# Attention values as plain fp32 matmuls in two column halves of the array, instead of split fp32r pairs

## The chip, the core and the metric

The kernel runs on one core of a Trainium2 chip. The core has a matmul engine (TensorE: PE in the profile, PEld for its weight loads), a vector engine (VectorE, DVE), a scalar engine (ScalarE, ACT), GpSimd (POOL) and a queue engine that here only issues transfers (SyncE, SP). Matmuls read SBUF and accumulate in PSUM banks of 512 fp32 columns. The metric is device time of one execution in microseconds (us), the median of three runs. The profile comes from one more execution, whose own time is given beside it.

## The reference, cut to what matters

One decoder layer on 512 positions: an input projection, two token mixers, two branch projections merged by gates, an output projection and a layer norm. The part that is changed is in mixer A, an attention with 8 heads in two groups (a group shares keys and values, 64 wide). With 512 positions, 8 selected blocks of 64 and a window of 512, both the selected-block branch and the window branch are plain causal attention, each with its own keys, values and gate:

```python
ss = jnp.einsum('bghqd,bgqld->bghql', qr, ksel) * scale
ps = masked_softmax(ss, msel[:, :, None])
o_slc = jnp.einsum('bghql,bgqld->bghqd', ps.astype(vsel.dtype), vsel)
...
sw = jnp.einsum('bghqd,bgkd->bghqk', qr, kw) * scale
pw = masked_softmax(sw, mw)
o_win = jnp.einsum('bghqk,bgkd->bghqd', pw.astype(vw.dtype), vw)
return gt[..., 0:1] * o_cmp + gt[..., 1:2] * o_slc + gt[..., 2:3] * o_win
```

So for each query tile of 128 positions the result is a sum over both branches and over all key tiles up to its own, of probabilities times values, with the gate multiplied into the probabilities.

## The kernel before, in words

Almost all matmuls take operands in fp32r, a form that the array takes at the full rate. Accuracy is kept by splitting each operand into a high part (a cast to fp32r, on ScalarE) and a low part (the difference, on VectorE) and by running two or three matmuls per product. The weights are streamed: `load` (L256) brings a raw 128x1024 block by an SP transfer into a pool of two buffers `wraw`, `weights` (L272) makes `whi` on ScalarE and `wlo` on VectorE, and `proj` (L318) runs 24 matmuls of 512 columns into a bank `pa`.

What isn't projection is written as Python generators. `_Weave` (L98) advances all of them by a tick after every six projection matmuls, and each `yield n` is a wait of n ticks. The numbers are in the table `D`. A tick only fixes the order in which instructions are written; every engine then runs its own instructions in that order, as fast as its inputs come. SP also issues its transfers in the order written, and a transfer that waits holds back those behind it.

The attention is cut into six units (L694), written u0 to u5 below: query tile 3 with branch 0 and with branch 1 (u0, u1), query tile 2 likewise (u2, u3), query tile 1 with both (u4), query tile 0 with both (u5). For each unit:

- `attn_scores` (L698): matmuls of queries and keys into banks `pss` and `pst`, in two halves of two heads a group (the halves are called a and b below), then on VectorE the masked scores and their row extreme (L729).
- `soften` (L737): exponentials with row sums on ScalarE (L745), reciprocal and gate on VectorE (L750, L753), and the probabilities multiplied by gate over sum, half of them on VectorE (L763) and half on ScalarE (L761).
- VectorE transposes 32x32 blocks into the one buffer `big` (L773), and 16 SP transfers of 32 partitions each (L784) exchange the blocks into the buffer `turn`, after which the keys lie on the partitions.
- `values` (L791), once for each pair of branch and key tile, 20 times in all: the block of `turn` is split (cast on ScalarE L200, difference on VectorE L202), and four matmuls of 512 columns, high and low part for each of two column blocks `ab`, go into two banks `pso`. The values `vv` are a fp32r array in which the 64 high and the 64 low columns of a group lie side by side; a matmul multiplies these 128 columns by the high or the low probabilities of that group, so that a bank holds the two parts of one group's result in two halves of its partitions.
- after the last pair of a query tile the halves are added up by copies on ScalarE (L810) and additions on VectorE (L814 to L817) into `asum`.

`turn` has one buffer, so the transfers of a unit wait until the matmuls of the unit before have read it (L777). `weave.claim` keeps two generators from taking the matmul engine in adjacent ticks. The compressed branch (`cmp_hidden`, `cmp_kv`, `cmp_scores`) runs beside it; its hidden layer (L567) is 32 plain fp32 matmuls with 64 weight columns each, two at a time in the two column halves of the array (weight columns 0 to 63 and 64 to 127), in two visits of 16.

Of the kernel before, what the change touches and what calls it, by code (L numbers as in the profile page):

```python
# [9 lines left out]
F32 = mybir.dt.float32  # L10
# [8 lines left out]
P = 128  # L19
# [19 lines left out]
SEQ = "kcmp kslc v q0 q1 q2 q3 kwin vcmp zb0 zb1 zb2 zb3 za0 za1 za2 za3".split()  # L39
# [10 lines left out]
def _columns(name):  # L50

    c = np.arange(_COLS[name], _COLS[name] + 128)
    if name[0] == "q" and name[1] != "b" or name[:2] == "za":
# [16 lines left out]
D = dict(h0=6, h2=5, h3=14, h4=0, h5=7, h6=10, n0=5, n1=2, n2=7, c0=2, c1=0, c2=0, c3=4, r0=5, p0=1, p1=13, p2=0,  # L70
         s0=1, s2=11, s3=0, v0=1, v1=11, v2=5, v3=9, e0=4, e1=2, t0=5, t1=4, t2=5, t3=3, t4=0, a5=4, y=2, w0=3, w1=1,
         x0=0, x1=0, e2=0, e3=3, o0=0, o1=6, o2=0)
D.update({"x0.za0": 2, "o0.0": 1, "t2.5": 4, "w0.35": 0, "y.m.1": 0, "o0.7": 1, "e3.2.2": 2, "y.o.3": 6, "o1.1": 3,
# [57 lines left out]
def layer_kernel(ctx: ExitStack, tc: tile.TileContext, xT, xn, w0, wi, wf, wv, small, brow, consts,  # L131
# [20 lines left out]
    t4 = ctx.enter_context(tc.tile_pool(name="t4", bufs=3))  # L152
    big = ctx.enter_context(tc.tile_pool(name="big", bufs=1))
    turn = ctx.enter_context(tc.tile_pool(name="turn", bufs=1))
# [8 lines left out]

    def T4():
        return t4.tile([P, 1024], F32R, name="t4", tag="t4")
# [138 lines left out]
    vv = cst.tile([P, 4, 2, 256], F32R, name="vv")  # L304
# [77 lines left out]
    def values_of(tt, ps):  # L382
        v = T2(NV)
        V.tensor_tensor(v, ps[:, 0:NV], brv, ALU.add)
        yield D["y"]
        vd = vv[:, tt].rearrange("p b (g c) -> p b g c", c=64)
        v4 = v[:, 0:256].rearrange("p (b g c) -> p b g c", b=2, c=64)
        G.tensor_copy(gat[:, tt], v[:, 256:NV])
        vts.append(vv[:, tt])
        yield from split_steps(v4, vd[:, :, 0:4:3], vd[:, :, 1:3], "v", tt)  # L390
# [170 lines left out]
    def cmp_kv():  # L561
# [5 lines left out]
        for j in range(16):  # L567
# [3 lines left out]
            if j == 7:  # L571
                yield 1
# [122 lines left out]
    turned, spent, finished, accs = [0], [0], [0], {}  # L695
# [41 lines left out]
    def soften(u, ms, ts, mn, den):  # L737
# [16 lines left out]
        for odd in range(2):  # L754
            for ab in range(2):
                for z, m in enumerate(ms):
                    for x in range(nb):
                        c, h = slice(n * x, n * x + n), (ab * nm + z) * nb + x
                        if z % 2 == odd:
                            if odd:  # L760
                                A.mul(ts[m, ab][:, c], ts[m, ab][:, c], den[:, h:h + 1])  # L761
                            else:
                                V.tensor_scalar(ts[m, ab][:, c], ts[m, ab][:, c], den[:, h:h + 1], None, ALU.mult)  # L763
            if odd == 0:
                yield wait_of("e3", u, ms[0])
# [9 lines left out]
        if ms[-1] == 3:  # L775
            yield wait_of("t3", u)
            while spent[0] < u:  # L777
                yield 1
# [12 lines left out]
    def values(u, st, lo):  # L791
# [5 lines left out]
        if (br, j) == (0, 0):  # L797
            accs[i] = PO(), PO()
# [5 lines left out]
        if st == (i + 1) * len(brs) - 1:  # L804
            spent[0] += 1
# [386 lines left out]
```

## Time and profile before

| what | value |
|---|---|
| median of three runs | 415.39 us (414.49 to 415.79) |
| the profiled execution's own time | 415.07 us |
| its span in the profile | 413.3 us |
| TensorE | 405.7 us busy, 98% of the span |
| VectorE | 313.5 us busy, 76% |
| ScalarE | 238.6 us busy, 58% |
| granted TensorE clock | 0.998 |

The page lists busy time by engine, then the costliest groups of instructions by line. A group's line reads: line, engine, operation, out<-in, shapes, count, busy time, mean duration of one in ns, idle time before it and what ended that. Matmul durations overlap, since the next starts before the last has drained, so a matmul's price is read from the distance between starts. A plain fp32 matmul leaves two records in the trace, a fp32r matmul one.

### The profile page before, as it was taken

The page shows a single profiled execution, that of the slowest core. Times are in us where ns is not written, and L with a number is a line of the kernel's source. Part 1 is how long each engine was busy: PE and PEld are TensorE (multiplying, and loading weights), DVE is VectorE, ACT ScalarE, POOL GpSimd, SP SyncE. Part 2 cuts the span into 40 slices and gives each one's busy share as a digit, 9 for nine tenths or more (in the row PEclk, how much of TensorE's full clock was granted, in tenths as well). Part 3 has the DMA queues.
Part 4 walks back from the last instruction along what each step waited for, and adds up shares of the span by engine and source line. Part 5 has one row for each costly group of instructions (what it writes and reads, how often), then busy time and mean ns, then how long its engine had stood idle before and what let it go on. Part 6 is the DMA issues. An engine that isn't in the chain of part 4 may idle for free.

```text
span 413.3 us, 5929 instructions
## 1 busy us (share of the span) xinstructions
PE 405.7 (98%) x2047; PEld 332.5 (80%) x2047; DVE 313.5 (76%) x641; ACT 238.6 (58%) x466; POOL 5.0 (1%) x18
## 2 busy tenths in 40 slices
PE   8999999999999999999999999999999999999994
PEld 8888888899888877877877777778878888888884
DVE  5916499878477688989998987589783899882773
ACT  4445552624247576767678595577864777637211
POOL 2000000001000000000000000000000000000000
PEclk9999999999999999999999999999999999999999
DMA  8965800333223424861166370655865752045131
GB/s 263 375 232 204 295 21 14 119 100 104 74 80 105 127 76 126 214 198 51 52 164 193 99 208 0 173 184 138 221 194 165 263 196 101 0 118 188 39 114 52
DMA packets 26542, 58.26 MB, mean 141 GB/s; under 512 B 5264, under 2 KB 7184, under 8 KB 26512
## 3 DMA queue, kind: packets, MB, share of 16 engines
q1 hardware_dynamic: 26080, 57.49, 44.8%
q8 instruction: 16, 0.26, 0.3%
q10 hardware_dynamic: 432, 0.39, 0.3%
q14 instruction: 14, 0.11, 0.1%
HBM read 42.12 MB, written 2.10 MB: 107 GB/s over the span
## 4 chain that ended last, share of the span: by engine, by line
PE 89%; DVE 5%; SPq 3%; issue 1%; ACT 1%; DMA 1%; DVEq 0%; ACTq 0%
PE pa L139 58%; PE pss L139 15%; PE pso L139 11%; PE pst L139 5%; SPq L146 3%; DVE turn L202 2%; DVE big L773 2%; DMA turn<-big 1%; ACT t L200 1%; PE pst L143 0%; DVE big L1111 0%; DVE wlo L277 0%; DVE asum L833 0%; ACT t L1106 0%; DVE big L1108 0%
## 5 line engine op out<-in xcount | busy, mean ns | idle before, releaser
L139 PE MATMUL pa<-t,whi 128*128 128x512 f32 x640 | 199.4, 393 | 0.0
L139 PEld LDWEIGHTS pa<-t,whi 128*128 128x128 f32 x640 | 118.6, 188 | 29.5 <-issue 5.3
L139 PE MATMUL pa<-t,wlo 128*128 128x512 f32 x320 | 124.7, 390 | 0.0
L277 DVE TENSOR_TENSOR wlo<-wraw,whi 128x1024 fp32r<-128x1024 f32 x44 | 53.4, 1216 | 26.8 <-ACT whi L274 25.8
L139 PEld LDWEIGHTS pa<-t,wlo 128*128 128x128 f32 x320 | 60.1, 188 | 12.8
L274 ACT CAST whi<-wraw 128x1024 fp32r<-128x1024 f32 x44 | 45.9, 1047 | 34.6 <-PE pa L139 16.6
L745 ACT ACTIVATE t<-t,sm_mn 128x512 f32<-128x512 f32 (+3 forms) x64 | 35.2, 551 | 11.9 <-DVE sm_mn L729 11.9
L139 PE MATMUL pso<-t,t 128*128 128x512 f32 (+2 forms) x158 | 33.0, 346 | 0.0
L139 PE MATMUL pss<-t,t 128*128 128x512 f32 (+2 forms) x158 | 30.2, 324 | 0.0
L773 DVE STREAM_TRANSPOSE big<-t 128x512 f32<-128x512 f32 (+2 forms) x48 | 25.8, 590 | 5.3 <-DMA turn<-big 3.4
L139 PEld LDWEIGHTS pso<-t,t 128*128 128x128 f32 x158 | 25.5, 194 | 3.7
L202 DVE TENSOR_TENSOR turn<-turn,t 128x1024 fp32r<-128x1024 f32 x20 | 23.4, 1208 | 6.1 <-ACT t L200 6.1
L139 PE MATMUL pa<-t,t 128*128 128x512 f32 (+1 forms) x104 | 27.3, 368 | 0.0
L139 PEld LDWEIGHTS pss<-t,t 128*128 128x128 f32 x158 | 23.8, 190 | 2.8
L200 ACT CAST t<-turn 128x1024 fp32r<-128x1024 f32 x20 | 20.0, 1051 | 8.7 <-DMA turn<-big 4.5
L139 PEld LDWEIGHTS pa<-t,t 128*128 128x128 f32 x104 | 18.5, 189 | 3.1
L200 ACT CAST t<-t 128x512 fp32r<-128x512 f32 x16 | 9.9, 617 | 18.7 <-DVE t L1003 11.4
L139 PE MATMUL pa<-turn,t 128*128 128x512 f32 x64 | 19.9, 389 | 0.0
L139 PE MATMUL pss<-t,whi 128*128 128x512 f32 x64 | 19.7, 389 | 0.0
L761 ACT ACTIVATE t<-t,sm_dn 128x512 f32<-128x512 f32 (+3 forms) x32 | 15.7, 554 | 5.4 <-DVE sm_dn L753 5.3
L729 DVE CUSTOM_DVE_ANT_0 t<-pss,t 128x512 f32<-128x512 f32 (+3 forms) x32 | 14.1, 485 | 4.8 <-PE pss L139 4.6
L139 PE MATMUL pso<-turn,vv 128*128 128x512 f32 x40 | 16.5, 412 | 0.7 <-DVE turn L202 0.6
(198 smaller groups left out, 564.0 us busy)
## 6 DMA issues: line engine op xcount, KB each, us to landing
wraw<-in_wf_dram SPq DMA_DIRECT2D x38, 512.0 KB, 3.7
turn<-big SPq DMA_DIRECT2D x48, 128.0 KB, 2.4
wraw<-in_wbr_dram SPq DMA_DIRECT2D x8, 512.0 KB, 4.3
t<-in_wout_dram SPq DMA_DIRECT2D x16, 256.0 KB, 4.3
t<-t SPq DMA_DIRECT2D x48, 64.0 KB, 2.0
turn<-big SPq DMA_DIRECT2D x32, 96.0 KB, 2.2
t<-in_wi_dram SPq DMA_DIRECT2D x8, 256.0 KB, 5.0
big<-in_w_dram SPq DMA_DIRECT2D x8, 256.0 KB, 6.7
```

The lines of the kernel that those rows point to most:

```text
L139: return tc.keep_in_program_order(nc.tensor.matmul(*a, **k))
L146: tc.keep_in_program_order(nc.sync.dma_start(o, i))
L200: A.copy(dst_hi, src)
L202: V.tensor_tensor(dst_lo, src, dst_hi.bitcast(F32), ALU.subtract)
L274: A.copy(hi, raws[i])
L277: V.tensor_tensor(lo, raws[i], hi.bitcast(F32), ALU.subtract)
L729: V.tensor_tensor_reduce(out=p[:, c], in0=dsts[m, ab][:, c], in1=amask[:, 512 - n:512], op0=ALU.add, op1=ALU.min, scale=-0.125, scalar=3.0e38,
L745: A.activation(p[:, c], p[:, c], AF.Exp, bias=mn[:, h:h + 1], scale=-1.0, accum_out=den[:, h:h + 1])
L761: A.mul(ts[m, ab][:, c], ts[m, ab][:, c], den[:, h:h + 1])
L773: V.transpose(view[:, :, :, 4 * ab + m], ts[m, ab][:, 0:128 * nst].rearrange("p (c b s) -> p c b s", b=4, s=32))
```

## The change

The values are kept as they are in plain fp32, and so are the turned probabilities. Both splits, the arrays `vv` and `t4`, and the two-bank sums go. `values` runs once a query tile, four times in all, over all its pairs of branch and key tile: for each pair two plain fp32 matmuls with 64 weight columns, group 0 into partitions 0 to 63 and group 1 into partitions 64 to 127 of one bank. That bank is then added to `asum` by one VectorE instruction, or copied there by ScalarE for the first query tile. `turn` gets two buffers, and the transfers of a unit wait for the matmuls of the unit before the last.

Three other things change with it. The multiplication of the probabilities by gate over sum can be shared out by a number `g`, and as `g` is set all of it is on ScalarE. The hidden layer of the compressed branch runs in one visit. The projection of `vcmp` comes ahead of `kwin`, and the table `D` of waits has other numbers (two of its lines are shown).

```diff
-SEQ = "kcmp kslc v q0 q1 q2 q3 kwin vcmp zb0 zb1 zb2 zb3 za0 za1 za2 za3".split()
+SEQ = "kcmp kslc v q0 q1 q2 q3 vcmp kwin zb0 zb1 zb2 zb3 za0 za1 za2 za3".split()
...
-D = dict(h0=6, h2=5, h3=14, h4=0, h5=7, h6=10, n0=5, n1=2, n2=7, c0=2, c1=0, c2=0, c3=4, r0=5, p0=1, p1=13, p2=0,
+D = dict(h0=6, h2=5, h3=14, h4=1, h5=7, h6=10, n0=5, n1=1, n2=6, c0=2, c1=5, c2=0, c3=3, r0=5, p0=1, p1=17, p2=0,
...
-    t4 = ctx.enter_context(tc.tile_pool(name="t4", bufs=3))
-    turn = ctx.enter_context(tc.tile_pool(name="turn", bufs=1))
+    turn = ctx.enter_context(tc.tile_pool(name="turn", bufs=2))
...
-        vd = vv[:, tt].rearrange("p b (g c) -> p b g c", c=64)
-        v4 = v[:, 0:256].rearrange("p (b g c) -> p b g c", b=2, c=64)
         G.tensor_copy(gat[:, tt], v[:, 256:NV])
-        vts.append(vv[:, tt])
-        yield from split_steps(v4, vd[:, :, 0:4:3], vd[:, :, 1:3], "v", tt)
+        vts[tt] = v
...
-            if j == 7:
-                yield 1
...
-        for odd in range(2):
-            for ab in range(2):
-                for z, m in enumerate(ms):
-                    for x in range(nb):
-                        c, h = slice(n * x, n * x + n), (ab * nm + z) * nb + x
-                        if z % 2 == odd:
-                            if odd:
-                                A.mul(ts[m, ab][:, c], ts[m, ab][:, c], den[:, h:h + 1])
-                            else:
-                                V.tensor_scalar(ts[m, ab][:, c], ts[m, ab][:, c], den[:, h:h + 1], None, ALU.mult)
-            if odd == 0:
-                yield wait_of("e3", u, ms[0])
+        parts_ = [(m, ab, slice(n * x, n * x + n), (ab * nm + z) * nb + x)
+                  for ab in range(2) for z, m in enumerate(ms) for x in range(nb)]
+        share = len(parts_) * wait_of("g", u, ms[0]) // 8
+        for m, ab, c, h in parts_[:share]:
+            V.tensor_scalar(ts[m, ab][:, c], ts[m, ab][:, c], den[:, h:h + 1], None, ALU.mult)
+        yield wait_of("e3", u, ms[0])
+        for m, ab, c, h in parts_[share:]:
+            A.mul(ts[m, ab][:, c], ts[m, ab][:, c], den[:, h:h + 1])
...
-            while spent[0] < u:
+            while spent[0] < u - 1:
                 yield 1
...
-            for st in range(nst):
-                part = w[:, 0:1024 * nst].rearrange("p (a c x) -> p c a x", a=4, x=256)[:, st]
-                weave.start(values(u, st, part), wait_of("t4", u) * st)
-
-    def values(u, st, lo):
-        i, brs = units[u]
-        br, j = brs[st // (i + 1)], st % (i + 1)
-        hi = T4().rearrange("p (a x) -> p a x", a=4)
-        yield from split_steps(lo.bitcast(F32), hi, lo, "u", u)
-        yield wait_of("t2", u)
-        if (br, j) == (0, 0):
-            accs[i] = PO(), PO()
-        for ab in range(2):
-            for k, t in enumerate((hi, lo)):
-                T.matmul(accs[i][ab], vts[j][:, br, 128 * ab:128 * ab + 128],
-                         t[:, :, 128 * ab:128 * ab + 128],
-                         start=(br, j) == (0, 0) and k == 0, stop=(br, j) == (1, i) and k == 1)
...
+            probs[u] = w.bitcast(F32)[:, 0:1024 * nst].rearrange("p (a c x) -> p c a x", a=4, x=256)
+            if brs[-1] == 1:
+                yield from values(u)
+
+    def values(u):
+        i = units[u][0]
+        yield from weave.claim(D["t2"])
+        tiles = [(v, st) for v in (u - 1, u) if units[v][0] == i for st in range(len(units[v][1]) * (i + 1))]
+        acc = PO()
+        for n, (v, st) in enumerate(tiles):
+            br, j = units[v][1][st // (i + 1)], st % (i + 1)
             for ab in range(2):
-                own, other = slice(64 * ab, 64 * ab + 64), slice(64 - 64 * ab, 128 - 64 * ab)
-                A.copy(o[own], acc[ab][other])
...
+                r = slice(64 * ab, 64 * ab + 64)
+                T.matmul(acc[r], vts[j][:, 128 * br + 64 * ab:128 * br + 64 * ab + 64],
+                         probs[v][:, st, :, 128 * ab:128 * ab + 128], start=n == 0, stop=n == len(tiles) - 1)
+        spent[0] = u + 1
+        acc = acc.rearrange("p (a m s) -> p a m s", a=4, m=4)
+        dst = asum[:, :, 128 * i:128 * i + 128].rearrange("p m (a s) -> p a m s", a=4)
+        if "sum" in ready:
+            V.tensor_tensor(dst, dst, acc, ALU.add)
+        else:
+            A.copy(dst, acc)
+        finished[0] += 1
```

Where instructions go can be seen in each engine's written order, before and after. On TensorE, around the first visit of the values (the operand `turn` or, before, also `vv`; `t_952` to `t_1066` are the values of the four key tiles; `pa` rows are projection matmuls), before:

```order
L139 MATMUL pa<-t_300,whi 128x512
L139 MATMUL pa<-t_299,wlo 128x512
L139 MATMUL pso<-t_1984,vv 128x512
L139 MATMUL pso<-turn,vv 128x512
L139 MATMUL pso<-t_1984,vv 128x512
L139 MATMUL pso<-turn,vv 128x512
L139 MATMUL pa<-t_114,whi 128x512
```

and now:

```order
L142 MATMUL pa<-t_199,wlo 128x512
L142 MATMUL pso<-turn,t_952 64x512 x2
L142 MATMUL pso<-turn,t_982 64x512 x2
L142 MATMUL pso<-turn,t_1014 64x512 x2
L142 MATMUL pso<-turn,t_1066 64x512 x2
L142 MATMUL pso<-turn,t_952 64x512 x2
L142 MATMUL pso<-turn,t_982 64x512 x2
L142 MATMUL pso<-turn,t_1014 64x512 x2
L142 MATMUL pso<-turn,t_1066 64x512 x2
L142 MATMUL pa<-t_224,whi 128x512
```

Four matmuls for one pair of branch and key tile, with projections before and behind, have become two plain fp32 matmuls for each of eight pairs in one row, between the same projections.

On SP, around the transfers of u1 (`turn_2169` before, `turn_2090` now; x16 are the sixteen transfers of a unit, `wraw` rows are weight loads), before:

```order
L146 DMA turn_1787<-big_1239 32x1024 x16
L146 DMA wraw_1816<-in_wf_dram 128x1024
L146 DMA wraw_1896<-in_wf_dram 128x1024
L146 DMA t2_1968<-in_consts_dram 128x512
L146 DMA wraw_1979<-in_wf_dram 128x1024
L146 DMA wraw_2042<-in_wf_dram 128x1024
L146 DMA wraw_2132<-in_wf_dram 128x1024
L146 DMA turn_2169<-big_1239 32x1024 x16
L146 DMA wraw_2220<-in_wf_dram 128x1024
```

and now:

```order
L149 DMA turn_1779<-big_1305 32x1024 x16
L149 DMA wraw_1804<-in_wf_dram 128x1024
L149 DMA wraw_1887<-in_wf_dram 128x1024
L149 DMA t2_1935<-in_consts_dram 128x512
L149 DMA wraw_1957<-in_wf_dram 128x1024
L149 DMA wraw_2055<-in_wf_dram 128x1024
L149 DMA turn_2090<-big_1305 32x1024 x16
L149 DMA wraw_2143<-in_wf_dram 128x1024
```

The transfers of u1 stand one weight load earlier, right behind `wraw_2055`, which takes the buffer that `wraw_1887` had.

On VectorE that buffer is given free by the row that makes `wlo_2123` (`t2_1989` to `t2_1995` are the masked scores of u2's half a, `t2_1980` and `t2_2014` belong to the compressed branch). From the row that follows the masked scores:

```order
L201 TENSOR_TENSOR t2_1894<-t2_1443,t2_1893 128x512
L669 STREAM_TRANSPOSE t2_2014<-t2_1934 128x512
L885 SCALAR_TENSOR_TENSOR t2_1985<-t2_1986,t2_1985 128x512
L670 TENSOR_REDUCE sm_mx_2015<-t2_2014 128x16
L677 TENSOR_REDUCE sm_mx_1981<-t2_1980 128x16
L671 TENSOR_TENSOR t2_2014<-t2_2014,sm_mx_2015 128x512
L678 RECIPROCAL sm_mx_1981<-sm_mx_1981 128x16
L885 SCALAR_TENSOR_TENSOR t2_1937<-t2_1938,t2_1937 128x512
L680 TENSOR_TENSOR sm_mx_1981<-sm_mx_1981,gc_369 128x4x4
L743 RECIPROCAL sm_dn_1961<-sm_dn_1961 128x4
L276 TENSOR_TENSOR wlo_2123<-wraw_1887,whi_2035 128x1024
```

That row now stands behind the masked scores of u2's half a and behind both reductions of the compressed branch; before, it stood ahead of those masked scores.

More of the change, by code (lines that the diff above doesn't have):

```diff
@@ L67 @@
     0, 128, 256, 260, 772, 1284, 1796, 2308, 2820)
-D = dict(h0=6, h2=5, h3=14, h4=0, h5=7, h6=10, n0=5, n1=2, n2=7, c0=2, c1=0, c2=0, c3=4, r0=5, p0=1, p1=13, p2=0,
-         s0=1, s2=11, s3=0, v0=1, v1=11, v2=5, v3=9, e0=4, e1=2, t0=5, t1=4, t2=5, t3=3, t4=0, a5=4, y=2, w0=3, w1=1,
-         x0=0, x1=0, e2=0, e3=3, o0=0, o1=6, o2=0)
-D.update({"x0.za0": 2, "o0.0": 1, "t2.5": 4, "w0.35": 0, "y.m.1": 0, "o0.7": 1, "e3.2.2": 2, "y.o.3": 6, "o1.1": 3,
[18 rows of a table removed]
+D = dict(h0=6, h2=5, h3=14, h4=1, h5=7, h6=10, n0=5, n1=1, n2=6, c0=2, c1=5, c2=0, c3=3, r0=5, p0=1, p1=17, p2=0,
+         s0=6, s2=8, s3=0, v0=0, v1=11, v2=5, v3=7, e0=4, e1=2, t0=5, t1=9, t2=4, t3=4, a5=4, y=2, w0=3, w1=0, x0=0,
+         x1=0, e2=0, e3=1, g=0, o0=0, o1=4, o2=0)
+D.update({"x0.za0": 2, "o0.0": 1, "w0.35": 0, "y.m.1": 0, "o0.7": 2, "y.o.3": 5, "o1.1": 3, "h2.0": 4, "w0.11": 2,
[21 rows of a table added]
 def wait_of(step, *at):
@@ L162, in T2 @@
         return t2.tile([P, n], dt, name="t2", tag="t2")
-    def T4():
-        return t4.tile([P, 1024], F32R, name="t4", tag="t4")
     def BIG():
@@ L302, in layer_kernel @@
     kcB = cst.tile([P, 32], F32, name="kcB")
-    vv = cst.tile([P, 4, 2, 256], F32R, name="vv")
     asum = cst.tile([P, 4, 512], F32, name="asum")
@@ L694, in layer_kernel @@
     units = [(i, brs) for i in range(3, -1, -1) for brs in (((0,), (1,)) if i >= 2 else ((0, 1),))]
-    turned, spent, finished, accs = [0], [0], [0], {}
+    turned, spent, finished, probs = [0], [0], [0], {}
     blocks = []
@@ L786, in soften @@
             yield wait_of("t1", u)
-            for st in range(nst):
-                part = w[:, 0:1024 * nst].rearrange("p (a c x) -> p c a x", a=4, x=256)[:, st]
-                weave.start(values(u, st, part), wait_of("t4", u) * st)
-    def values(u, st, lo):
-        i, brs = units[u]
-        br, j = brs[st // (i + 1)], st % (i + 1)
-        hi = T4().rearrange("p (a x) -> p a x", a=4)
-        yield from split_steps(lo.bitcast(F32), hi, lo, "u", u)
-        yield wait_of("t2", u)
-        if (br, j) == (0, 0):
-            accs[i] = PO(), PO()
-        for ab in range(2):
-            for k, t in enumerate((hi, lo)):
-                T.matmul(accs[i][ab], vts[j][:, br, 128 * ab:128 * ab + 128],
-                         t[:, :, 128 * ab:128 * ab + 128],
-                         start=(br, j) == (0, 0) and k == 0, stop=(br, j) == (1, i) and k == 1)
-        if st == (i + 1) * len(brs) - 1:
-            spent[0] += 1
-        if (br, j) == (1, i):
-            acc, o = accs[i], T2()
-            for ab in range(2):
-                own, other = slice(64 * ab, 64 * ab + 64), slice(64 - 64 * ab, 128 - 64 * ab)
-                A.copy(o[own], acc[ab][other])
-                s, t = (x.rearrange("p (a m s) -> p a m s", a=4, m=4) for x in (o, acc[ab]))
-                dst = asum[own, :, 128 * i:128 * i + 128].rearrange("p m (a s) -> p a m s", a=4)
-                if "sum" in ready:
-                    V.tensor_tensor(o[own], o[own], acc[ab][own], ALU.add)
-                    V.tensor_tensor(dst, dst, s[own], ALU.add)
-                else:
-                    V.tensor_tensor(dst, s[own], t[own], ALU.add)
-            finished[0] += 1
@@ L851, in layer_kernel @@
     oa = [None] * 4
-    vi, vts, wis = [], [], []
+    vi, vts, wis = [], {}, []
     bri, brv = T2(), T2(NV)
@@ L891, in cmp_tile @@
         yield from cmp_hidden(a, de)
-    qraw = []
+    qraw = {}
     def q_tile(m, ps, b):
-        qraw.append(evac(ps, b))
+        qraw[m] = evac(ps, b)
         yield from queries(m, qraw[m])
@@ L936, in layer_kernel @@
             weave.start(z_tile(name, ps, m), wait_of("x0", name))
-    wo, woraw = [], {}
+    wo, woraw = {}, {}
     def load_out(kt):
@@ L970, in split_out @@
             V.scalar_tensor_tensor(lo, raw, nm, hi.bitcast(F32), ALU.add, ALU.subtract)
-        wo.append(hl)
+        wo[kt] = hl
     def out_ahead(n):
```

39 rows, old and new, of tables (x0, x1) are left out of this document.

## Prediction

> **What bounds the kernel now.** I read the busy times first, then what TensorE waits for, then one stretch of the middle.
>
> ```profile
> PE 405.7 (98%) x2047; PEld 332.5 (80%) x2047; DVE 313.5 (76%) x641; ACT 238.6 (58%) x466; POOL 5.0 (1%) x18
> ...
> PE pso L139 <- DVE t L212: 1.1, 1, 1.1
> PE pso L139 <- DVE turn L202: 0.6, 2, 0.4
> ...
> 186.00:235.00 49.00, 48.60 (x257) 37.05 (x242) 47.05 (x94) 35.02 (x62) 0.00 (x0) 1.00 0.37 104
> ```
>
> The second and third rows are all that TensorE waits for: 1.1 us at the start and 0.6 us for the low halves of turned blocks. The last gives busy time between 186 and 235 us: TensorE 48.60 of 49, VectorE 47.05, ScalarE 35.02. So the end is the sum of the matmuls' prices plus small waits, but from 186 to 235 VectorE has only 2 us to spare and can become the bound at any wait for its result. Time off VectorE or ScalarE counts only where it ends a TensorE wait; time off TensorE counts fully, unless a new wait takes it back. Prices come from distances of starts. In the chain of waits:
>
> ```profile
> 195.80 1.13 PE pso L139 x4
> ...
> 199.68 0.93 PE pso L139 x4
> ...
> 205.69 0.74 PE pss L139 x6
> 206.42 0.53 PE pst L139 x6
> ...
> 283.91 16.35 PE pa L139 x72
> ```
>
> A projection matmul costs 16.35/72 = 0.227 us, four values matmuls 0.93, twelve score matmuls 0.74 + 0.53 = 1.27.
>
> **Values before.** 20 times four matmuls at 0.93 is 18.6. Beside that come waits for the low half:
>
> ```profile
> 230.46 0.40 PE L139 MATMUL pso<-t,vv 128*128 128x512 f32 x1
> 231.26 0.50 PE L139 MATMUL pso<-turn,vv 128*128 128x512 f32 x1 [0.40 <-DVE turn L202]
> 231.59 0.39 PE L139 MATMUL pso<-t,vv 128*128 128x512 f32 x1
> ...
> 251.58 0.40 PE L139 MATMUL pso<-t,vv 128*128 128x512 f32 x1
> 252.00 0.50 PE L139 MATMUL pso<-turn,vv 128*128 128x512 f32 x1
> ...
> 274.58 0.40 PE L139 MATMUL pso<-t,vv 128*128 128x512 f32 x1
> 275.15 0.50 PE L139 MATMUL pso<-turn,vv 128*128 128x512 f32 x1 [0.17 <-DVE turn L202]
> ...
> 302.90 0.40 PE L139 MATMUL pso<-t,vv 128*128 128x512 f32 x1
> 303.37 0.50 PE L139 MATMUL pso<-turn,vv 128*128 128x512 f32 x1
> ```
>
> The four distances are 0.80, 0.42, 0.57 and 0.47 instead of 0.23, so 1.34 too long; the matmul after each restart starts 0.11 late (231.26 to 231.59), 0.44 in all; a visit right behind scores takes 1.13 (the row at 195.80), 0.2 more, and for this and the like I count 0.6. Sum: 18.6 + 1.3 + 0.4 + 0.6 = 20.9, say 21.
>
> **Values after.** There are 20 pairs of plain fp32 matmuls, one in each column half, of 512 columns. The trace has no such pair; the two nearest rows:
>
> ```profile
> 150.54 0.40 PE L139 MATMUL pa<-t,wlo 128*128 128x512 f32 x1
> 150.87 1.97 PE L139 MATMUL pss<-big,t 128*64 128x128 f32 x32
> 152.77 0.73 PE L139 MATMUL pa<-t,whi 128*128 128x512 f32 x2
> 153.34 0.39 PE L139 MATMUL pa<-t,wlo 128*128 128x512 f32 x1
> ...
> 185.44 1.09 PE L139 MATMUL pss<-t,kcB 64*32 64x512 f32 x16
> 186.46 0.72 PE L139 MATMUL pa<-t,whi 128*128 128x512 f32 x2
> ```
>
> The first visit is the hidden layer: 32 records are 16 matmuls, eight pairs in column halves with 128 columns each, from start to the next start 1.90. The second is eight fp32 matmuls of 512 columns, all beside each other in eight tiles, 1.02. I take a visit as a fixed part S plus c for each 128 columns of what runs after each other: 1.90 = S + 8c and 1.02 = S + 4c give c = 0.22 and S = 0.14. A pair of 512 columns is then 4c = 0.88. Each visit adds S, and what the rows show beside it: 0.10 at its entry (150.54 to 150.87 instead of 0.23) and 0.11 at its exit (152.77 to 153.34 instead of 0.46), 0.35 in all, four times: 1.4. So 20 × 0.88 + 1.4 = 19.0. Bounds for the pair: below, if entry and exit already sit in the 1.02 of the second visit, 1.02 − 0.21 = 0.81, which makes 17.6; above, if the fixed part comes with every pair, 1.02, which makes 21.8. The rows have 512 columns in eight tiles and 128 columns in halves, so both sizes that the change joins are there, and I take what they solve to. Values: 21.0 to 19.0, **−2.0**.
>
> A sentence of the Trainium skill speaks against the change: "TensorEngine Tiling (Array Packing)", Key Properties, says that a change of tiling mode drains TensorE. The rows agree with a loss, of 0.35 per visit, which in twenty visits would be 7.0; the change has four.
>
> The hidden layer in one visit instead of two drops one entry and exit: **−0.35**.
>
> **Off TensorE.** VectorE loses its differences, additions and multiplications:
>
> ```profile
> L202 DVE TENSOR_TENSOR turn<-turn,t 128x1024 fp32r<-128x1024 f32 x20 | 23.4, 1208 | 6.1 <-ACT t L200 6.1
> L814 DVE TENSOR_TENSOR t<-t,pso 64x512 f32<-64x512 f32 x8 | 5.5, 684 | 0.6 <-ACT t L810 0.4
> L763 DVE TENSOR_SCALAR t<-t,sm_dn 128x512 f32<-128x512 f32 x8 | 3.5, 483 | 0.1
> L200 ACT CAST t<-turn 128x1024 fp32r<-128x1024 f32 x20 | 20.0, 1051 | 8.7 <-DMA turn<-big 4.5
> L761 ACT ACTIVATE t<-t,sm_dn 128x512 f32<-128x512 f32 (+3 forms) x32 | 15.7, 554 | 5.4 <-DVE sm_dn L753 5.3
> ```
>
> That is 23.4, 5.5, about as much again for the additions of the same shape behind them (L815), and 32 multiplications at 0.48 or less: about 44 us, less the four adds. ScalarE loses 20.0 of casts and takes on another 32 multiplications, 15.7. Both are covered by TensorE, so I price this at nothing by itself; it pays only by making VectorE earlier.
>
> **The new waits.** The first values visit needs the probabilities of u0 and u1. TensorE's written order puts it 96 projection matmuls and three score groups behind the scores with `kcB`. These start at 185.44, now earlier by the 0.35 and by six projections (1.36): 183.7; with 1.0 of their own, 96 × 0.227 = 21.8, 3 × 1.27 = 3.8 and about 0.9 of restarts, TensorE is there at **211.2**. The transfers of u1 stand on SP behind the load `wraw_2055`, whose buffer VectorE frees with `wlo_2123`. VectorE today:
>
> ```profile
> 183.82 0.88 DVE L763 TENSOR_SCALAR t<-t,sm_dn 128x512 f32<-128x512 f32 x2
> ...
> 188.23 2.31 DVE L202 TENSOR_TENSOR turn<-turn,t 128x1024 fp32r<-128x1024 f32 x2
> 190.47 1.28 DVE L668 TENSOR_TENSOR t<-pss,t 128x512 f32<-128x512 f32 x2
> 191.67 1.21 DVE L277 TENSOR_TENSOR wlo<-wraw,whi 128x1024 fp32r<-128x1024 f32 x1
> 192.80 1.22 DVE L202 TENSOR_TENSOR turn<-turn,t 128x1024 fp32r<-128x1024 f32 x1
> ...
> 195.13 0.67 DVE L677 TENSOR_REDUCE sm_mx<-t 128x16 f32<-128x512 f32 x1
> 195.73 0.68 DVE L905 SCALAR_TENSOR_TENSOR t<-t,t 128x512 f32<-128x512 f32 x1
> ...
> 258.22 11.42 SPq L146 DMA_DIRECT2D turn<-big  x16
> 283.94 10.04 SPq L146 DMA_DIRECT2D turn<-big  x16
> ...
> 271.43 2.00 ACT L200 CAST t<-turn 128x1024 fp32r<-128x1024 f32 x2
> ...
> 295.92 2.00 ACT L200 CAST t<-turn 128x1024 fp32r<-128x1024 f32 x2 [1.59 <-DMA turn<-big]
> ```
>
> The compressed adds (L668) start 5.0 us after the `kcB` scores; 2.2 of subtractions (188.23 to 190.47) and 0.8 of multiplications ahead of them go: 183.7 + 2.0 = 185.7. From there to `wlo_2123` the new order has thirteen rows of the kind that takes 0.60 (195.13 to 195.73; the adds are two of them), two weight differences at 1.13 (191.67 to 192.80), and four masked scores and five small ones, for which I take 2.4 together: 12.5, so 198.2. SP then issues the load, and the transfers from 198.7 (half a us is my guess). Sixteen transfers take from first issue to first use 12.0 (283.94 to the cast at 295.92, which waited for them); elsewhere up to 13.2 (258.22 to the cast at 271.43, whose wait other work may have lengthened). So the probabilities are there at 210.7 to 211.9 and the **wait is 0 to 0.7**. Every us that VectorE is later here is a us of TensorE. u4's transfers may start only when the second visit has read the buffer; TensorE comes to the third about 13.0 later (48 projections, scores, restarts), a wait of 0 to 0.2. By the same count of matmuls the transfers of u0, u2 and u3 are there well before their visits, and those of u5 a little before. I take **+0.6** for all, near the upper end of u1's wait. What queues behind these waits are projections, and behind SP's stalled load the next weight loads, which in both orders come two blocks ahead.
>
> Sum: −2.0 − 0.35 + 0.6 = −1.75. The profiled execution took 415.07 and becomes 413.3; the median lies 0.32 above it, so 413.6.
>
> **Rivals.**
> - *No new wait.* VectorE is early enough at u1: −2.35, 413.0; with the pair at its lower bound −3.75, 411.6. For it: some 40 us off VectorE. Against: the 12.5 us of VectorE that now stand ahead of a load which stands ahead of the transfers.
> - *u1's transfers come late, by 1.2 to 3.5 us of TensorE's wait.* If VectorE reaches the compressed adds as late as now (5.0 after the scores instead of 2.0), the wait is 3.0 to 3.7. The sum is 415.39 − 2.35 + 1.2 to 3.5: 414.2 to 416.5, no change that can be told. For it: VectorE is 47.05 of 49 busy there, and u1's transposes on it, which stand ahead of the adds, now wait for multiplications that are all ScalarE's.
> - *Slower: ScalarE is late.* The place is the same. u1 has four multiplications more on ScalarE in each half, 8 × 0.55 = 4.4 (the L761 row); if none of it is hidden, transposes, `wlo_2123`, SP and TensorE are 4.4 later, and with the 0.6 the sum is 415.39 − 2.35 + 5.0 = 418.0. It decides from a wait of 3.6 on. Against: ScalarE is busy 35 of 49 there, and loses about eight casts of 1.05 in the same stretch.
> - *The halves overlap badly.* If a quarter of the second half isn't hidden, a pair is 0.88 × 1.25 = 1.10, the values 22.0 + 1.4 = 23.4, +2.4, and the sum 415.39 + 2.4 − 0.35 + 0.6 = 418.0; halves one after the other would add 17.6. Against: the hidden layer's eight pairs fit in 1.90, so 128 columns take 0.24 at most; but no row has 512 columns in halves. By the Trainium skill, "TensorE: Matmul & The Clock Gate", Part 3, three column tiles bring 2.38 times the rate of one, 79% of the ideal; by that a pair is an estimated 1.11 and the sum about 418.2, which the hidden layer's rows don't bear out.
>
> **How the numbers follow.** Chances: forecast, with waits of 0.2 to 1.2, 0.44; no wait 0.15; late transfers 0.28; ScalarE late 0.09; bad overlap 0.04. A measurement of this kernel tells 0.3%, 1.25 us, from no change: faster is below 414.15, slower above 416.65. The first two cases are faster (0.59), the third the same (0.28), the last two slower (0.13). The forecast by itself is 413.2 to 414.2. The range takes in the low end of the pair nearly to its bound and all of the third case, 411.8 to 416.6, and leaves out the slower ones.
>
> **What will show it.** Visits of 16, 12, 8 and 4 matmuls of about 7.2, 5.4, 3.7 and 1.9 us from start to next start; pairs 0.88 apart. `wlo_2123` on VectorE near 198; the first `turn` row of SP for u1 near 199; the first visit on TensorE near 211 with a wait under 1 us named after `turn`. VectorE's busy time near 270. The forecast is wrong if the pairs lie over 1.0 apart, if the first or third visit waits over 1.2 us, or if a new wait for `whi` or `wlo` shows.

## The result and the profile after

The changed kernel takes 412.37 us (411.66 to 412.86, four runs) against 415.15 (414.49 to 415.79): a ratio of 0.9932, 95% interval 0.9909 to 0.9954, so 2.8 us faster. The profiled execution took 412.86 with a span of 410.7, against 415.07 and 413.3.

From the page of the changed kernel, its busy times and two groups (columns as for the rows of before):

```profile
PE 403.8 (98%) x2047; PEld 323.2 (79%) x2047; DVE 272.2 (66%) x576; ACT 227.0 (55%) x467; POOL 5.4 (1%) x18
...
L754 ACT ACTIVATE t<-t,sm_dn 128x512 f32<-128x512 f32 (+3 forms) x64 | 30.6, 552 | 2.8 <-DVE sm_dn L746 2.7
...
L142 PE MATMUL pso<-turn,t 128*64 128x512 f32 x80 | 18.0, 597 | 0.0
```

VectorE fell from 313.5 to 272.2 us, ScalarE from 238.6 to 227.0: its multiplications rose from 15.7 to 30.6 us, and 20.0 of casts are gone (the two rows of before are in the prediction). The 40 values matmuls leave 80 records. Then all that TensorE waits for:

```profile
PE pso L142 <- DVE t L211: 1.1, 1, 1.1
```

and the stretch from 186 to 235 us:

```profile
186.00:235.00 49.00, 49.00 (x250) 34.59 (x249) 35.39 (x88) 32.48 (x69) 0.00 (x0) 1.00 0.50 140
```

Only the wait at the start is left, and VectorE is busy 35.39 of the 49 us, where it had been 47.05.

The first values visit, on TensorE's timeline:

```profile
211.11 0.39 PE L142 MATMUL pa<-t,wlo 128*128 128x512 f32 x1
211.43 7.09 PE L142 MATMUL pso<-turn,t 128*64 128x512 f32 x32
218.44 0.73 PE L142 MATMUL pa<-t,whi 128*128 128x512 f32 x2
219.02 0.39 PE L142 MATMUL pa<-t,wlo 128*128 128x512 f32 x1
```

The visit of 16 matmuls (32 records) takes 7.01 from its start to the next start, entry 0.32 instead of 0.23 and exit 0.58 instead of 0.46. Inside it the starts of a pair's two matmuls lie 0.007 apart and pairs 0.857 apart, the first pair 0.05 and the last 0.10 longer. A visit thus costs 0.857 a pair and 0.36 beside them (0.09 + 0.15 + 0.12); the four visits make 20 × 0.857 + 4 × 0.36 = 18.6. Before, the same distances of starts add up to 21.2 for the 80 matmuls.

What stands ahead of it, on VectorE and SP:

```profile
185.99 1.29 DVE L661 TENSOR_TENSOR t<-pss,t 128x512 f32<-128x512 f32 x2
...
197.10 1.19 DVE L276 TENSOR_TENSOR wlo<-wraw,whi 128x1024 fp32r<-128x1024 f32 x1
...
198.74 11.30 SPq L149 DMA_DIRECT2D turn<-big  x16
...
211.76 0.58 DVE L762 STREAM_TRANSPOSE big<-t 128x384 f32<-128x384 f32 x1 [0.61 <-DMA turn<-big]
```

The compressed adds start at 185.99, `wlo_2123` at 197.10, the transfers of u1 at 198.74. The last row is the next writer of `big`; it waited until 211.76 for these transfers, so they had landed by about then. TensorE, which began its visit at 211.43, did not wait.

### The profile page after: what moved, and what is told of

Read it like the earlier page. It is cut to its first block, busy times and chain, and to the rows that moved or that the text cites. A ratio compares the mean times of both kernels' runs of the same rounds, so it can differ in the third digit from the quotient of the medians.

```text
span 410.7 us, 5846 instructions
## 1 busy us (share of the span) xinstructions
PE 403.8 (98%) x2047; PEld 323.2 (79%) x2047; DVE 272.2 (66%) x576; ACT 227.0 (55%) x467; POOL 5.4 (1%) x18
## 4 chain that ended last, share of the span: by engine, by line
PE 98%; DVE 1%; issue 0%; DVEq 0%; ACT 0%; ACTq 0%
PE pa L142 65%; PE pss L142 15%; PE pso L142 12%; PE pst L142 5%; PE pst L146 0%; DVE big L1091 0%; DVE t L549 0%; DVE t L201 0%; DVE big L1088 0%; DVEq L1168 0%; ACT t L1086 0%; DVE t L211 0%; DVE sm_ss L1089 0%; DVEq L276 0%; ACTq L1086 0%
## 5 line engine op out<-in xcount | busy, mean ns | idle before, releaser
L754 ACT ACTIVATE t<-t,sm_dn 128x512 f32<-128x512 f32 (+3 forms) x64 | 30.6, 552 | 2.8 <-DVE sm_dn L746 2.7
L142 PE MATMUL pso<-turn,t 128*64 128x512 f32 x80 | 18.0, 597 | 0.0
L142 PE MATMUL pst<-t,t 128*128 128x512 f32 (+2 forms) x80 | 15.1, 345 | 0.0
L142 PEld LDWEIGHTS pst<-t,t 128*128 128x128 f32 x80 | 13.0, 189 | 1.9
```

The costliest lines, as they stand in the source:

```text
L142: return tc.keep_in_program_order(nc.tensor.matmul(*a, **k))
```

## Experiments

Ratios below are against the kernel before, measured again beside each run; the changed kernel's time is 412.37. Two theories were held against each other at first. **Theory 1** is that of the prediction: TensorE needs u1's blocks when the first visit begins. **Theory 2** came from the profile after: the visit reads u0's four blocks first, 4 × 0.857 = 3.4 us, so u1's are needed only at 214.9, some 3.1 after they came.

### More work on VectorE ahead of the transfers (inconclusive)

```diff
+        for _ in range(4):
+            V.tensor_tensor(idle, amask[:, 0:512], amask[:, 0:512], ALU.add)
         for g in range(2):
             V.tensor_tensor(sT[g], pg[g], cmask, ALU.add)
```

Four:

> The changed kernel with four idle VectorE additions of 128x512 (some 0.60 us each, 2.4 us in all, into a tile that nobody reads) ahead of the two adds of the compressed scores, that is ahead of wlo_2123, of the load behind it and of u1's transfers. Nothing is left out. Theory 1 (the prediction's): TensorE needs u1's blocks when the first values visit begins, so 2.4 us more on VectorE are 2.4 us more of TensorE: a wait of 2.0 to 2.4 at the first visit, time 414.4 to 414.8 against 412.37. Theory 2: the visit reads u0's four blocks first, four pairs of 0.857 = 3.4 us, so u1's blocks, there at about 211.7, are needed at 214.9 only and 3.1 us are to spare: no wait over 0.3 us, time within 0.6 of 412.4.

Ten:

> The same with ten idle additions, 6.0 us. Nothing is left out. Theory 1: a wait of about 6 us at the first visit, time near 418.2. Theory 2: 6.0 minus 3.1 to spare, a wait of about 2.9 us inside the first visit, between its fourth and its fifth pair, time near 415.2. If VectorE's lateness shows first elsewhere (a score bank or a wlo that TensorE needs), the wait is named after that and both theories lack a term.

Measured: 412.46 (ratio 0.9941, 0.9929 to 0.9953) and 412.29 (0.9936, 0.9923 to 0.9949). Neither theory was put to the test. On VectorE's timeline of the kernel with ten additions:

```profile
21.86 2.87 DVE L662 TENSOR_TENSOR idle<-t 128x512 f32<-128x512 f32 x4 [1.55 <-DMA t<-in_consts_dram]
30.45 1.41 DVE L662 TENSOR_TENSOR idle<-t 128x512 f32<-128x512 f32 x2
32.38 2.86 DVE L662 TENSOR_TENSOR idle<-t 128x512 f32<-128x512 f32 x4
```

The additions, written ahead of the adds that run at 186 us, depend on nothing late, and they ran at 22 to 35 us, where they cost nothing. So VectorE's order is not that of the ticks alone: it is put together when the program is built, and what depends on nothing late can move forward. Work that is to delay a place must depend on something that comes just ahead of it.

### The later unit first

```diff
-        tiles = [(v, st) for v in (u - 1, u) if units[v][0] == i for st in range(len(units[v][1]) * (i + 1))]
+        tiles = [(v, st) for v in (u, u - 1) if v >= 0 and units[v][0] == i for st in range(len(units[v][1]) * (i + 1))]
```

> Four idle additions (2.4 us) as before, and in each values visit the pairs of the later unit come first, so that u1's blocks are needed when the visit begins. Nothing is left out. Theory 2: u1's blocks come at about 211.7 + 2.4 = 214.1, TensorE is there at 211.4: a wait of about 2.7 us ahead of the first pair, time near 415.1. Theory 1 doesn't care for the order inside the visit and gives the same wait here as in the kernel with four idle additions alone. A third possibility, that the idle additions are hidden behind something else, gives no wait in both.

Measured: 413.19, ratio 0.9950 (0.9938 to 0.9962). The four additions stood at the start of the program here too, so this kernel tests only the order inside the visit. TensorE's timeline:

```profile
210.98 0.39 PE L142 MATMUL pa<-t,wlo 128*128 128x512 f32 x1
212.24 7.09 PE L142 MATMUL pso<-turn,t 128*64 128x512 f32 x32 [0.86 <-DMA turn<-big]
```

With u1's blocks needed first, a wait as in the prediction is there: 0.86 us, named after the transfers, and the time is some 0.8 higher. The 2.7 that theory 2 expected here had the 2.4 us of additions in it, which did not delay anything. In the changed kernel the order of the pairs hides the wait.

### Later transfers

```diff
+            for e in range(4 * (u == 1)):
+                dma(idle[32 * (e % 4):32 * (e % 4) + 32, 128 * (e // 4):128 * (e // 4) + 128], consts[0:32, K_SM:K_SM + 128])
             for a in range(4):
                 for b in range(4):
                     dma(to[32 * b:32 * b + 32, a], of[32 * a:32 * a + 32, b])
```

Four:

> The changed kernel with four small transfers (32x128, from a constant into a tile that nobody reads) on SP right ahead of u1's sixteen; each row of SP takes about 0.6 us, so u1's transfers start about 2.4 us later. The extra tile is the only other difference; nothing is left out. Theory 1 (the prediction's): TensorE needs u1's blocks at the start of the first visit: a wait of 2 to 2.4 us, time near 414.7. Theory 2: u0's four blocks are read first, 3.4 us; the last of u1's lands at 211.7 + 2.4 = 214.1 and is needed at 214.9: no wait, time within 0.6 of 412.4.

Ten:

> The same with ten small transfers, about 6 us. Nothing is left out. Theory 1: a wait of about 6 us, time near 418. Theory 2: 6.0 less the 3.1 to spare, a wait of about 2.9 us, and it stands inside the first visit, between its fourth and its fifth pair; time near 415.2. If the weight load behind u1's transfers is what TensorE waits for, the wait is named after whi or wraw instead.

Measured: 412.11 (ratio 0.9933, 0.9919 to 0.9948) and 414.35 (0.9979, 0.9970 to 0.9988). SP and TensorE of the kernel with ten:

```profile
198.23 4.59 SPq L149 DMA_DIRECT2D idle<-in_consts_dram  x10
202.87 10.84 SPq L149 DMA_DIRECT2D turn<-big  x16
...
210.92 3.65 PE L142 MATMUL pso<-turn,t 128*64 128x512 f32 x16
215.74 3.65 PE L142 MATMUL pso<-turn,t 128*64 128x512 f32 x16 [1.17 <-DMA turn<-big]
```

A small transfer holds SP 0.46 us, not 0.6. The last of u1's transfers leaves SP at 213.71 (202.87 + 10.84), in the changed kernel at 210.04 (198.74 + 11.30): 3.7 later, and TensorE is 0.5 earlier, so the two are 4.2 closer. The visit breaks exactly between its fourth and fifth pair, and the second part starts 1.34 after the place where it would have (210.92 + 3.48 = 214.40). So 4.2 − 1.3 = 2.9 us were to spare. Theory 2 holds, theory 1 has fallen. Four transfers cost nothing, as theory 2 says.

### The halves one after the other

```diff
-        for n, (v, st) in enumerate(tiles):
-            br, j = units[v][1][st // (i + 1)], st % (i + 1)
-            for ab in range(2):
-                r = slice(64 * ab, 64 * ab + 64)
+        for ab in range(2):
+            r = slice(64 * ab, 64 * ab + 64)
+            for n, (v, st) in enumerate(tiles):
+                br, j = units[v][1][st // (i + 1)], st % (i + 1)
```

> The values matmuls in another order: in each visit first all pairs' matmuls into the lower column half, then all into the upper one, so that no two neighbours lie in different halves. Nothing is left out. If it is the overlap of the halves that makes a pair cost 0.857, a single matmul costs 0.857 and the 40 of them 34.3 instead of 17.1: +17.1 us, near 429.5. If a plain fp32 matmul with 64 weight columns is cheaper by itself (0.43 each), nothing changes.

Measured: 422.38 in a single run (before 415.06), some 10 us over the changed kernel. TensorE:

```profile
210.84 12.29 PE L142 MATMUL pso<-turn,t 128*64 128x512 f32 x32
223.06 0.73 PE L142 MATMUL pa<-t,whi 128*128 128x512 f32 x2
```

The visit takes 12.22 instead of 7.01. Its records in one half lie 0.429 apart, two for each matmul, so one plain fp32 matmul alone costs 0.857 (a fp32r one 0.227), and the pair costs what one does: the overlap of the halves is whole, and the rival of a badly overlapping pair is refuted. 17.1 was expected, though, and 10.4 came by the distances of starts. Where the order passes from the lower to the upper half, records lie in four close couples, 0.005 to 0.058 apart, where one half alone has 0.429: the first four of the upper half run beside the last four of the lower. TensorE overlaps halves beyond direct neighbours, here by about 1.7 us a visit.

### Eight visits for one query tile

```diff
         for n, (v, st) in enumerate(tiles):
+            if n and i == 3:
+                yield 1
```

> The changed kernel with the eight pairs of query tile 3 in eight visits, six projection matmuls between each two; the other query tiles as they are. What follows in the attention is some 7 ticks later in the written order. Nothing is left out. Theory: each further visit costs what the rows around a visit show, 0.09 at its entry, 0.15 in it and 0.12 behind it, 0.36: seven more are +2.5 us of TensorE, time near 414.9. Rival: the 0.36 is the price of a restart behind something awaited and not of the change between column halves and the whole array; then the eight visits cost under 0.7 more together, time within 0.9 of 412.4.

Measured: 421.79, ratio 1.0166 (1.0152 to 1.0180): 9.4 over the changed kernel, not 2.5. TensorE's timeline at the first two visits, and where it waited:

```profile
210.97 1.08 PE L142 MATMUL pso<-turn,t 128*64 128x512 f32 x4
211.98 0.73 PE L142 MATMUL pa<-t,whi 128*128 128x512 f32 x2
...
213.57 0.65 PE L142 MATMUL pso<-turn,t 128*64 128x512 f32 x2
...
344.87 0.50 PE L142 MATMUL pa<-t,whi 128*128 128x512 f32 x1 [3.20 <-ACT t L199]
346.59 0.80 PE L142 MATMUL pa<-t,whi 128*128 128x512 f32 x1 [1.21 <-DVE t L201]
```

From visit to visit it is 2.60; six projections are 1.36 and the pair 0.857, which leaves 0.38: the price of a visit holds (0.36), and seven more are 2.7. These visits wait for nothing, so the rival, by which the 0.36 is a restart behind something awaited, has fallen. The Trainium skill, "TensorEngine Tiling (Array Packing)", Key Properties, has a change of tiling mode drain TensorE; the trace agrees with a loss at each visit, these 0.38. The rest of the 9.4 comes much later: at 341 to 347 TensorE stands still for 3.20 and 1.21 us, which by starts (3.59 and 1.71 instead of 0.23 each) costs 4.8, and then runs at half its clock (below), another 1.4. The attention ends later in the written order here; that this brings the two waits is likely, but not shown.

### The split matmuls in the four visits

```diff
-                T.matmul(acc[r], vts[j][:, 128 * br + 64 * ab:128 * br + 64 * ab + 64],
-                         probs[v][:, st, :, 128 * ab:128 * ab + 128], start=n == 0, stop=n == len(tiles) - 1)
+                for k in range(2):
+                    T.matmul(accs[ab], vts[j][:, br, 128 * ab:128 * ab + 128],
+                             probs[v][:, st, :, 128 * ab:128 * ab + 128],
+                             start=n == 0 and k == 0, stop=n == len(tiles) - 1 and k == 1)
```

> The changed kernel with the values matmuls of the kernel before, in the four visits of the change: the values are split into high and low columns again (that split is there), and for each pair four fp32r matmuls of 128 columns go into two banks. The split of the turned probabilities is left out: both matmuls of a group read the unsplit block, and one bank is left unread. So it has TensorE's work of the kernel before without the casts, differences and waits. Theory A: what the change gains is the 20 entries and waits of before; 80 fp32r matmuls in four visits cost 80 x 0.227 = 18.2 against 18.6 in the changed kernel: time 412.0, within 0.6 of 412.4. Theory B: the plain fp32 halves are cheaper on TensorE by themselves; then this goes back towards 414.8.

Measured: 412.31, ratio 0.9937 (0.9923 to 0.9951). TensorE:

```profile
210.52 0.39 PE L142 MATMUL pa<-t,wlo 128*128 128x512 f32 x1
210.75 7.63 PE L142 MATMUL pso<-turn,vv 128*128 128x512 f32 x32
218.21 0.62 PE L142 MATMUL pa<-t,whi 128*128 128x512 f32 x2
```

The visit is 7.46 and loses nothing at its entry and exit, and the 80 matmuls are 18.7 by starts, as the 18.6 of the change. Theory A holds: TensorE gains nothing from the plain fp32 halves themselves. They cost what four fp32r matmuls cost, without needing a split.

### The kernel before without the low halves

```diff
-        yield from split_steps(lo.bitcast(F32), hi, lo, "u", u)
+        A.copy(hi, lo.bitcast(F32))
+        yield wait_of("y", "u", u)
```

> The kernel before with the 20 differences of the turned blocks (the low halves, VectorE) left out: the second matmul of each group reads the unsplit block. That is all that is left out; TensorE's and SP's orders are word for word those of the kernel before. Theory A (gain from waits, not from the fp32 form): the four long gaps ahead of the low half and their restarts go, 1.3 + 0.4, and the 80 values matmuls cost 18.6 to 19.3 by starts instead of 21.2: time 413.0 to 413.6 against 415.1, most of the change's gain. Theory B (those gaps come from transfers and casts, which stay): under 0.6 faster.

Measured: 415.27, ratio 1.0003 (0.9989 to 1.0017): no gain. That is inside theory B's number, but not for its reason. At the values theory A is right: the four gaps are gone, and the 80 matmuls cost 19.1 instead of 21.2 by starts. But TensorE's timeline shows two waits that the kernel before does not have:

```profile
341.10 0.50 PE L139 MATMUL pa<-t,wlo 128*128 128x512 f32 x1 [0.40 <-DVE wlo L277]
...
343.62 0.50 PE L139 MATMUL pa<-t,whi 128*128 128x512 f32 x1 [0.39 <-DVE t L202]
```

and in the stretch around them (columns as above) VectorE is busy 10.00 of 10 us:

```profile
335.00:345.00 10.00, 9.22 (x40) 6.98 (x39) 10.00 (x17) 7.58 (x14) 0.00 (x0) 1.00 0.50 163
```

With their restarts they take 1.3 us of the 2.1 back. So what was gained at the values is partly paid again later, by waits for VectorE's results. The full VectorE alone doesn't explain them: it is busy 10.00 of these 10 us in the kernel before and in the changed one too, where TensorE does not wait. The remaining 0.8 doesn't show in the medians, and why not is open. (The profile hides it: after the same 26 matmuls at the start this execution stands at 6.98 us, that of the kernel before at 6.29 and that of the changed kernel with half of the multiplications back on VectorE at 5.90, so single executions differ that much there.) VectorE's built order had also moved with the 20 rows gone, so this is not a clean removal, and how much the change itself owes to its new order at 335 to 345 is open.

### The multiplications

In the kernel before, all on ScalarE:

```diff
-                            if odd:
+                            if True:
                                 A.mul(ts[m, ab][:, c], ts[m, ab][:, c], den[:, h:h + 1])
```

> The kernel before with all 64 multiplications of the probabilities on ScalarE, none on VectorE (as in the change). Nothing is left out and TensorE's and SP's orders stay. VectorE loses 10.4 us, ScalarE gains some 15. Theory A: the differences on VectorE come earlier and the waits ahead of the low halves (1.3 + 0.4) shrink by about half: 0.5 to 1.0 faster, near 414.4. Theory B: the casts of the turned blocks and the transposes now wait for ScalarE: the same or up to 2 us slower.

In the changed kernel, half of them back on VectorE (the number `g` from 0 to 4):

> The changed kernel with half of the multiplications back on VectorE (its number g at 4 instead of 0; one unit keeps its own setting). Nothing is left out, and the orders of TensorE and SP stay but for names. VectorE gains about 10 us over the span, ScalarE loses about 15. Theory 2 (u1's blocks have 3 us to spare, the other units no less): no new wait, time within 0.6 of 412.4. The prediction's view, in which each us of VectorE ahead of u1's transfers is a us of TensorE: four multiplications of some 0.45 more there, 1.8 us slower, near 414.2.

Measured: 417.80, ratio 1.0066 (1.0053 to 1.0080), for the first; 412.77, ratio 0.9944 (0.9930 to 0.9959), for the second. What TensorE waits for in the first, beside the start:

```profile
PE pso L139 <- DVE turn L202: 2.4, 4, 1.0
...
PE pss L139 <- DVE t L577: 0.6, 1, 0.6
```

and two of the four waits in the first row, on the timelines of ScalarE, SP, VectorE and TensorE:

```profile
247.64 3.31 ACT L761 ACTIVATE t<-t,sm_dn 128x256 f32<-128x256 f32 x8
...
251.43 2.93 ACT L200 CAST t<-turn 128x1024 fp32r<-128x1024 f32 x3
...
253.78 0.50 PE L139 MATMUL pso<-turn,vv 128*128 128x512 f32 x1 [0.76 <-DVE turn L202]
...
260.00 12.27 SPq L146 DMA_DIRECT2D turn<-big  x16
...
274.13 2.49 DVE L771 STREAM_TRANSPOSE big<-t 128x512 f32<-128x512 f32 x4 [3.46 <-DMA turn<-big]
276.54 1.18 DVE L202 TENSOR_TENSOR turn<-turn,t 128x1024 fp32r<-128x1024 f32 x1
277.78 0.50 PE L139 MATMUL pso<-turn,vv 128*128 128x512 f32 x1 [1.02 <-DVE turn L202]
```

VectorE has 10 us less to do over the span (303.7 busy instead of 313.5), and yet TensorE waits for its differences 2.4 us instead of 0.6. At 253.78 the difference waits for a cast, and the casts stand on ScalarE behind eight multiplications of 3.31 us, where the kernel before has four of 1.71. At 277.78 the difference stands on VectorE behind four transposes that write `big`, and these wait until the transfers of u3 have read it; these start 1.8 later than before (260.00 instead of 258.22), as TensorE by then is too, and in this execution they take 0.85 longer (12.27 instead of 11.42), for a reason that is open. So theory B holds, by somewhat more than it said. It does not have the other row of the waits: at 161 us a score matmul waits for a result of the compressed branch, which costs 0.9 by starts and was not taken apart. Of the 0.6 us that TensorE waits in the kernel before, 0.17 stand behind the same four transposes; the other 0.40 (at 231.26 there, 232.19 here) are the same with 10 us less work on VectorE, so VectorE's multiplications are not their cause. In the changed kernel no matmul waits for VectorE behind such transposes, and moving the multiplications has no effect that can be told: theory 2 again, and not the 414.2 of the prediction's view.

### The hidden layer in two visits

```diff
+            if j == 7:
+                yield 1
```

> The changed kernel with the hidden layer of the compressed branch in two visits of 16 matmuls again, six projection matmuls between them. Nothing is left out. The prediction's price of one visit says +0.35 us on TensorE by the distances of starts; a verdict of the time can hardly tell that (412.7 against 412.4).

Measured: 416.72, ratio 1.0044 (1.0029 to 1.0058): 4.3 over the changed kernel, instead of 0.35. By starts the hidden layer's records take 3.80 instead of 3.64, and with entry and exit the 0.35 is right. The rest shows in the timelines of ScalarE and TensorE:

```profile
160.51 1.04 ACT L273 CAST whi<-wraw 128x1024 fp32r<-128x1024 f32 x1 [3.80 <-PE pa L142]
161.46 0.68 ACT L883 ACTIVATE t<-pa,sml 128x512 f32<-128x512 f32 x1
162.04 0.68 ACT L885 ACTIVATE t<-pa,hbias 128x512 f32<-128x512 f32 x1
...
162.77 0.73 PE L142 MATMUL pa<-t,whi 128*128 128x512 f32 x2 [2.08 <-ACT t L885]
```

and in stretches of 1 us behind it (the eighth column is the granted clock):

```profile
163.00:164.00 1.00, 1.00 (x5) 0.77 (x5) 1.00 (x2) 0.88 (x2) 0.00 (x0) 0.82 0.57 160
164.00:165.00 1.00, 1.00 (x5) 0.35 (x3) 1.00 (x2) 0.00 (x0) 0.00 (x0) 0.50 0.00 0
...
167.00:168.00 1.00, 1.00 (x6) 0.59 (x5) 1.00 (x5) 0.66 (x2) 0.00 (x0) 0.97 0.90 330
```

One tick more put the cast of a weight block ahead of the two activations that empty a projection bank. The cast waits until TensorE is done with the buffer, and TensorE then waits for the bank: 2.46 from start to start. After that the clock is 0.50 for 3.4 us, which costs another 1.7. With the 0.35 of the visit that makes 0.35 + (2.46 − 0.23) + 1.7 = 4.3.

## Why the prediction was right, and where it was not

The forecast was 413.6, faster by 1.75 us; 412.37 came, faster by 2.8, inside the range and on the right side. Point by point:

- **Values after.** The sum took 0.88 a pair and 0.35 a visit, 19.0 in all. Measured are 0.857 and 0.36, 18.6. The two rows from which S and c were solved carried the answer to 3%. The kernel with the halves in turn shows that the overlap is whole. The Trainium skill, "TensorE: Matmul & The Clock Gate", Part 3, has three column tiles bring 2.38 times one; the 79% of the ideal that follows doesn't carry over to the two halves of 512 columns here, which bring 2.0 times one.
- **Values before.** The sum said 21.0; by starts it is 21.2. Together the term is −2.6, where −2.0 was written. It does not rest on the new matmuls, as the term could be read: the split matmuls in four visits cost as little. The gain on TensorE is that 1.3 us of gaps, their restarts and the small losses of 20 visits are gone.
- **Hidden layer.** −0.35 by the row before; the rows of the two-visit kernel bear it out.
- **New waits.** This is the step that failed. The times themselves were right to 0.3 us: compressed adds 185.7 against 185.99, `wlo_2123` done at 198.2 against 198.29, the transfers at 198.7 against 198.74, TensorE at 211.2 against 211.43. The need was put at the wrong place: "The first values visit needs the probabilities of u0 and u1" is true of the visit, but u1's come in its second half. With the two units exchanged, the wait is 0.86, a little over the 0 to 0.7 of the sum; as built it is 0, with 2.9 to spare. So +0.6 is 0, and "every us that VectorE is later here is a us of TensorE" holds only from 2.9 us on. The same was overlooked for u4: the second visit reads u2's blocks first, so u4's transfers could start at 272.18, inside that visit (268.55 to 273.85) and not after it, and the third visit did not wait either.
- **Sum.** With the measured sizes: −2.6 − 0.35 + 0 = −2.95, against −2.8 in the medians and −2.5 in the distances of starts of the two profiled executions. Part of what lies between is of single executions: of the changed one's, the first 7 us were 0.4 longer and a score group at 143 us 0.3. Against that, 96 matmuls of the values' projection (280 columns) lie 0.1285 apart instead of 0.133, 0.4 us. Nothing that was predicted does this. The split matmuls in four visits and the halves in turn ran at 0.133 again; its cause is open. No run holds the new table `D` or the new order of the projections apart from the rest; by starts, no other group of matmuls changed by more than 0.4.
- **Rivals.** "No new wait" at 413.0 is what came, and it had a chance of 0.15. The forecast is 1.2 too high: 0.6 for a wait that did not come and 0.6 for the values. Both errors point the same way, and the range held because it took in the low end of both. "u1's transfers come late" and "ScalarE is late" named the right place but took the slack for 0; for a wait of 3.6 the transfers would have had to be 6.5 us later than they were. Moving all multiplications to ScalarE does cost 2.8 us, but in the kernel before, where casts of the blocks stand behind them on ScalarE.

That VectorE's 41 us were priced at nothing by themselves stands: TensorE was busy at 98% before and after. The kernel before without its low halves warns, though, that a gain at one stage can be paid back at a later one.

## What to carry to other kernels

When a transfer feeds a long visit, ask which of its matmuls reads the block first; the spare time is the length of what stands ahead of it inside the visit. A plain fp32 pair in column halves costs here what four split fp32r matmuls cost (0.857 against 0.93), so what it saves here is casts, differences and the waits for them, as long as the pairs are gathered in few visits at some 0.36 us each. When a wait is taken away, look at the later stages with a full engine, where new waits can take the gain back. And look at the granted clock behind every long wait of TensorE: here one of 2.08 us halved it for a while, and single ones of up to 1.17 did not.

## What the runs showed of the hardware that was not expected

- **A long wait costs more than itself.** After a gap of 2.46 us between starts (hidden layer in two visits), and after one of 3.59 with one of 1.71 right behind it (eight visits), the granted clock fell to 0.50 for 3.4 us. That cost 1.7 us in the first kernel and 1.4 in the second, where part of the slow stretch fell into the wait. After gaps of 1.26, 1.42 and 1.76 us (later unit first, multiplications on ScalarE, ten transfers) it stayed at 1.00. What lies between 1.76 and 2.46 is not measured. From the kernel with eight visits:

```profile
346.00:347.00 1.00, 0.41 (x1) 0.41 (x2) 1.00 (x2) 1.00 (x4) 0.00 (x0) 0.60 0.85 246
347.00:348.00 1.00, 1.00 (x3) 0.75 (x3) 1.00 (x3) 1.00 (x4) 0.00 (x0) 0.50 0.90 348
```

  The Trainium skill, "TensorE: Matmul & The Clock Gate", Part 1, gives an idle window of about 3.4 us for this; here TensorE stood still for 2.08 us (2.46 from start to start), and that was enough.
- **Column halves overlap out of the written order.** With all lower matmuls written ahead of all upper ones, the first four records of the upper half ran beside the last four of the lower, which saved 1.7 us a visit. This is read from the distances of starts; the records don't name their half.
- **A small transfer (32x128) holds SP 0.46 us** (4.59 for ten), where one of a unit's sixteen holds it 0.63 to 0.76 (10.05 to 12.23 for sixteen, in the changed kernel).
